# Weights of every other index of the seven-product stage arrive in four free slots instead of the weight ring

## The chip, the core and the metric

The kernel runs on one core of one Trainium2 chip. The metric is the device time of one launch in microseconds. The engines meant below are TensorE (PE, matrix products, with its weight loads shown as PEld), VectorE (DVE), ScalarE (ACT), GpSimd (POOL), and SyncE (SP), whose queue issues nearly all DMA transfers. Each engine takes its instructions strictly in the order in which they were built.

## The reference

One inference step of a two-layer decoder trunk over 1040 prompt rows (16 learned ones and 1024 of the prompt) and 8 sequences of 4 sample rows, with a model width of 1024. Layer 0 has an S5 scan beside a short gated convolution, layer 1 a Conformer convolution module, and both end in a gated feed-forward block of width 2816:

```
def conv_ffn(xn, fbuf, p, l):
    u = xn @ p['w_ffn_up'][l]
    a, g = jnp.split(u, [D_FF], axis=-1)
    a_c, nbuf = causal_dwconv(a, fbuf, p['w_ffn_conv'][l])
    return (jax.nn.silu(a_c) * g) @ p['w_ffn_down'][l], nbuf
```

All data is 32-bit. The kernel keeps that precision by cutting every matrix operand into a high and a low part (`h` is the operand rounded to the matmul type, `l` the rest) and computing three products: `xh*wh`, `xl*wh`, `xh*wl`.

## The kernel before

The rows are worked on in two halves: half 0 has 512 rows, half 1 has 560 (528 prompt rows and the 32 sample rows). The feed-forward width is cut into 22 indices `f` of 128 columns, in groups `GROUPS` of 2, 4, 4, 4, 4 and 4. For each index the kernel makes `a` and `g` (`up`), the three-tap convolution of `a`, `h = silu(conv) * g`, and splits `h`; when a group is complete, `down` adds its product with `w_down` to the residual `xr`, in eight output tiles `m`.

The change lies in the last stage, half 1 of layer 1. There `a` and `g` of an index come from one two-by-two block product with seven block products instead of eight (`up7`). The 1024 input rows are two blocks of 512, and the 560 rows of the half are two blocks of 280; `prepare` forms the combinations of the activations once (`oh`, `ol`). For each index the two raw weight tiles, value `w_up[2f]` and gate `w_up[2f+1]`, each 128x1024 (512 KB), are seen as four halves of 128x512: `a11`, `a12`, `a21`, `a22`. DVE forms from them `s1 = a21+a22`, `s2 = s1-a11`, `s4 = a12-s2`, `s3 = a11-a21`. Seven weights, `a11`, `a12`, `s1`, `s2`, `s3`, `s4`, `a22`, are each split: the high part by ACT (`wh`, or `a22h`), the low part by DVE (`wl`, `a22l`). That is `hl`, and every split is of 128x512.

The seven products of an index (`product`, twelve matmuls of 280 columns each) go into three PSUM banks: `bx` collects `a11*B11`, then `s2*T2`, then `s3*T3`, then `a22*N4`; `by` collects `s1*T1`, then `s4*B22`; `bz` holds `a12*B21`. A bank is read between two products, before the next one is added to it: after the first product ACT copies `bx` to the first half of `ap` (the evacuation of the first product, L908) and `by` to `g` (L910), after `s2` ACT copies `bx` to the second half of `ap` (L916, L917), after `s4` DVE adds `by` to it. Then ACT and DVE do the convolution (`c`, L499 on ACT and two L501 on DVE), ACT the silu (`s`, L926, L927). After `s3` DVE adds `bx` to `g`; only then may the `a22` product be added to that bank. After it DVE multiplies it into `s` and `split` makes `hh` and `hl`, the operands of `down`.

Raw weights come through a ring of two buffers, tag `raw`, 4 KB per partition each, which the tiles of `w_down` (also 512 KB) share in the order of the program. So an index takes both buffers, and its transfers can be issued only when the splits and sums of the previous user have read the buffers. Split weights live in rings `wh`, `wl` of three. `slot("v", ...)` gives one of eight slots of 584 numbers per partition; in this stage they hold `ap` and `c` of each index (and `h` of two indices of the last group); when the stage begins they still hold the operands of half 0's last `down`. Five banks, tag `mm`, serve `up7` (three per index) and `down` (two per `m`).

The order of instructions on each engine is set when the program is built: the framework's scheduler simulates the program with its own costs and due times, and whatever it finds ready first stands first in the queue. At run time nothing is reordered. The loop that calls `up7` is `run` with the hooks `out0` (final scaling and output of half 0, tile `xr`, L1167, L1168) and `finals` (the tail).

Of the kernel before, what the change touches and what calls it, by code (L numbers as in the profile page):

```python
# [12 lines left out]
F32 = mybir.dt.float32  # L13
# [8 lines left out]
P = 128  # L22
# [15 lines left out]
FT = FF // P  # L38
# [22 lines left out]
def grp(lo, hi, n):  # L61
    return [list(range(f, f + n)) for f in range(lo, hi, n)]


GROUPS = grp(0, 2, 2) + grp(2, FT, 4)


def build(nc, tc, ctx, a):
    sm = ctx.enter_context(tc.tile_pool(name="sm", bufs=1))
    sl = ctx.enter_context(tc.tile_pool(name="sl", bufs=1))  # L70
    wp = ctx.enter_context(tc.tile_pool(name="wp", bufs=3))
    ps = ctx.enter_context(tc.tile_pool(name="ps", bufs=1, space=PSUM))
    dr = ctx.enter_context(tc.tile_pool(name="dr", bufs=1, space=DRAM))
    V, A, PL, PE, SY = nc.vector, nc.scalar, nc.gpsimd, nc.tensor, nc.sync
    COUNT = {"x": NXT, "xh": NXH, "t": NTT, "v": NVT}

    def slot(tag, name, shape, dt=F32):
        if isinstance(shape, int):
            shape = [P, TN[shape]]
        n = math.prod(shape[1:])  # L80
        assert n <= SW
        t = sl.tile([P, SW], dt, tag=tag, name=name, bufs=COUNT[tag])
        v = t[:shape[0], :n]
        if len(shape) > 2:
            n = " ".join(f"d{i}" for i in range(len(shape) - 1))
            v = v.rearrange(f"p ({n}) -> p {n}", **{f"d{i}": shape[i + 1] for i in range(len(shape) - 2)})
        return v
# [4 lines left out]
    def bank(name, tag="aux"):  # L92
        return ps.tile([P, 512], F32, tag=tag, name=name, bufs=BANKS[tag])
# [6 lines left out]
    def tt(o, x, y, op, e=V):  # L100
        return e.tensor_tensor(o, x, y, op=op)  # L101
# [53 lines left out]
    def split(src, name, hf, scale=None, tag="xh", t0=0):  # L155
        hl = h, l = [slot(tag, name + c, hf, F32R) for c in "hl"]
        src, h, l = [t[:, t0:] for t in (src, h, l)]
        if scale is None:
            A.activation(h, src, AF.Copy)  # L159
            tt(l, src, h.bitcast(F32), SUB)  # L160
        else:
            A.activation(h, src, AF.Copy, scale=scale)  # L162
            V.scalar_tensor_tensor(l, src, scale, h.bitcast(F32), op0=MUL, op1=SUB)  # L163
        return hl
# [6 lines left out]
    def ntok(hf):  # L171
        return TN[0] if hf == 0 else HP1
# [3 lines left out]
    def tick(us, mark):  # L176
        state["f"] += us * RATE
        with tc.issue_after(mark.ins), tc.issue_after(state["pe"].ins):
            while fills and state["f"] >= 1:
                r = next(fills[0], "end")  # L180
                if r == "end":
                    fills.pop(0)
                elif r is False:
                    state["f"] = 1
                    return
                else:
                    state["f"] -= 1
# [215 lines left out]
    def sj(t, o=HP1):  # L403
        return t[:, o:o + NS * DS].rearrange("p (s j) -> p s j", j=DS)
# [93 lines left out]
    def conv3(dst, src, w, n):  # L498
        A.activation(dst[:, :n], src[:, 0:n], AF.Copy, scale=w[:, 0:1])  # L499
        for k in (1, 2):  # L500
            mk = V.scalar_tensor_tensor(dst[:, :n], src[:, k:k + n], w[:, k:k + 1], dst[:, :n], op0=MUL, op1=ADD)  # L501
        return mk

    def s6(t, n):
        return t[:, n:n + 6 * NS].rearrange("p (s j) -> p s j", j=6)

    def last2(t, n):
        return t[:, n - 6:n + 6 * NS].rearrange("p (s j) -> p s j", j=6)[:, :, 4:6]
# [268 lines left out]
    class FFN:  # L777
# [77 lines left out]
        def up7(self, f, tag, htag, stag, atag):  # L855


            fw, n, H = self.fw[:, f], ntok(1), self.H
            o, M = 2 + n, P * KT // 2
            raws = []  # L860
            for i in range(2):
                raw = wp.tile([P, 1024], F32, tag="raw", name="raw", bufs=2)
                SY.dma_start(raw, a["w_up"][(self.layer * FT + f) * 2 + i])
                raws.append(raw)

            def ring():
                return [wp.tile([P, 1024], F32R, tag=t, name=t, bufs=WB) for t in ("wh", "wl")]

            def hl(hl_, raw):
                A.activation(hl_[0], raw, AF.Copy)  # L870
                tt(hl_[1], raw, hl_[0].bitcast(F32), SUB)
                return hl_

            def halves(w):
                return [[t[:, i * M:(i + 1) * M] for t in w] for i in range(2)]

            (a11, a12), (a21, a22) = [(t[:, :M], t[:, M:]) for t in raws]
            w11, w12 = halves(ring())
            hl(w11, a11)
            s1, s2, s3, s4 = [slot(stag, "s%d" % i, [P, M]) for i in range(1, 5)]  # L880
            tt(s1, a21, a22, ADD)
            ws1, ws2 = halves(ring())
            hl(ws1, s1)
            hl(w12, a12)
            tt(s2, s1, a11, SUB)
            hl(ws2, s2)
            tt(s4, a12, s2, SUB)
            ws4, ws3 = halves(ring())
            hl(ws4, s4)
            tt(s3, a11, a21, SUB)  # L890
            hl(ws3, s3)
            w22 = hl([slot(atag, "a22" + c, [P, M], F32R) for c in "hl"], a22)

            def product(b, w, x, start):
                for k, xk in enumerate(self.ops[x]):
                    for i in range(3):
                        state["pe"] = PE.matmul(  # L897
                            b[:, :H], w[i == 2][:, k * P:(k + 1) * P], xk[i == 1],
                            start=(start and k == 0 and i == 0), stop=(k == KT // 2 - 1 and i == 2),
                            skip_group_check=True)  # L900

            bx, by, bz = [bank("mm", "mm") for _ in range(3)]
            ap = slot(tag, "ap", [P, o + 6 * NS])
            PL.tensor_copy(ap[:, 0:2], self.carry[:, f])
            PL.tensor_copy(s6(ap, o)[:, :, 0:2], self.fin[:, f])
            g = slot("t", "g", [P, H])
            product(bx, w11, "B11", True)
            A.activation(ap[:, 2:2 + H], bx[:, :H], AF.Copy)  # L908
            product(by, ws1, "T1", True)
            A.activation(g, by[:, :H], AF.Copy)  # L910
            product(bz, w12, "B21", True)
            tt(ap[:, 2:2 + H], ap[:, 2:2 + H], bz[:, :H], ADD)
            product(bx, ws2, "T2", False)
            m = n - H
            sa, sp = s6(ap, o)[:, :, 2:6], ap[:, 2 + H:o]
            A.activation(sp, bx[:, :m], AF.Copy)  # L916
            A.activation(sa, sj(bx, m), AF.Copy)  # L917
            product(by, ws4, "B22", False)
            tt(sp, sp, by[:, :m], ADD)
            tt(sa, sa, sj(by, m), ADD)  # L920
            PL.tensor_copy(self.fout[:, f], last2(ap, o))
            nc_ = n + 6 * NS
            c = slot(tag, "c", [P, nc_ + 2])
            conv3(c, ap, fw, nc_)
            s = slot("t", "s", 1)
            A.activation(s[:, :n], c[:, :n], AF.Silu)  # L926
            A.activation(sj(s), s6(c, o)[:, :, 0:4], AF.Silu)  # L927
            self.flush()
            product(bx, ws3, "T3", False)
            tt(g, g, bx[:, :H], ADD)  # L930
            tick(84 * H / 2400, tt(s[:, H:], s[:, H:], g, MUL))
            h = {}

            def rest():
                product(bx, w22, "N4", False)
                tt(s[:, :H], s[:, :H], bx[:, :H], MUL)
                h[1] = split(s, "h", 1, tag=htag)

            self.pend = rest
            return h  # L940
# [439 lines left out]
```

## Time and profile before

| | |
|---|---|
| runs | 2243.32 us median of 3 (2242.76 to 2243.97) |
| profiled execution, its own time | 2242.73 us |
| span of that execution | 2240.9 us |
| mean granted TensorE clock | 0.990 |
| PE busy / DVE busy / ACT busy / POOL busy | 98% / 76% / 37% / 33% |
| first and last matmul of `product` (L897) | 1821.3 to 2174 us |

The profile is of one execution. Its page gives busy shares by engine and by fortieth of the span; the trace behind it has every instruction with its start, its duration and, where its engine stood idle before it, how long and for which event. A bracket such as `[2.03 <-ACT wh L870]` behind a row means that the engine was idle 2.03 us before this instruction and that ACT's write of `wh` at line 870 ended the idle time. PE rows overlap: a 280-column matmul lasts 0.29 us but the next one starts about 0.13 us later.

### The profile page before, as it was taken

The numbers are of one execution on the slowest core, as the hardware profiler recorded it, in microseconds if no ns is written. First come the engines' busy times: TensorE is split into PE (matmuls) and PEld (weight loads), VectorE is DVE, ScalarE is ACT, GpSimd is POOL, SyncE is SP. The second block draws the span as 40 slices with busy tenths as digits, with TensorE's granted clock in tenths as the row PEclk, the third lists the DMA queues.
The fourth block names the chain that finished last, engine by engine and source line by source line (L and its number), as shares of the span: only waits on it lengthen the run. The fifth ranks groups of instructions, "written<-read, shape, count | busy, mean of one in ns | idle before, by whom it ended". The sixth has DMA issues, their size and how long they took to land.

```text
span 2240.9 us, 34315 instructions
## 1 busy us (share of the span) xinstructions
PE 2185.1 (98%) x13504; PEld 1982.3 (88%) x13504; DVE 1694.9 (76%) x2872; ACT 827.9 (37%) x1255; POOL 734.3 (33%) x632
## 2 busy tenths in 40 slices
PE   7999999999999999999999999999999997999997
PEld 6888898888888889999999998888887987999997
DVE  8979966545544678888896789899998387878784
ACT  5122354322332423232234523333335343455452
POOL 3212114323333434333443426455454401110011
PEclk8999999999999999999999999999999999999998
DMA  5234541223222332222222353232322222333231
GB/s 170 94 97 132 187 142 50 94 94 94 94 94 94 94 94 86 85 85 85 85 77 93 94 109 99 94 94 85 112 86 87 84 76 94 113 95 95 87 105 61
DMA packets 98338, 218.07 MB, mean 97 GB/s; under 512 B 28417, under 2 KB 45185, under 8 KB 98177
## 3 DMA queue, kind: packets, MB, share of 16 engines
q1 hardware_dynamic: 97632, 215.37, 31.1%
q8 instruction: 106, 1.74, 0.3%
q10 hardware_dynamic: 544, 0.52, 0.1%
q14 instruction: 56, 0.45, 0.1%
HBM read 202.49 MB, written 13.36 MB: 96 GB/s over the span
## 4 chain that ended last, share of the span: by engine, by line
PE 76%; DVE 13%; issue 3%; DMA 3%; ACT 2%; POOL 1%; SPq 1%; POOLq 0%; ACTq 0%; DVEq 0%
PE mm L145 66%; PE mm L897 8%; DVE c L501 2%; DVE wl L101 1%; DMA raw<-w_up 1%; DVE cvb L1052 1%; DVE cva L1052 1%; DVE xr L101 1%; DMA x<-x 1%; DVE xnl L163 1%; DMA raw<-w_down 1%; DVE hl L101 1%; ACT wh L113 1%; DVE s L101 1%; PE bcs L253 1%
## 5 line engine op out<-in xcount | busy, mean ns | idle before, releaser
L101 POOL TENSOR_TENSOR wl<-raw,wh 128x1024 fp32r<-128x1024 f32 x181 | 444.2, 2454 | 662.0 <-ACT wh L113 619.9
L145 PE MATMUL mm<-xnh,wh 128*128 128x280 f32 (+3 forms) x2176 | 637.7, 337 | 6.7 <-ACT xnh L162 6.7
L145 PE MATMUL mm<-xnl,wh 128*128 128x280 f32 (+3 forms) x2176 | 641.2, 338 | 2.5 <-DVE xnl L163 2.5
L145 PE MATMUL mm<-xnh,wl 128*128 128x280 f32 (+3 forms) x2176 | 639.3, 338 | 0.0
L113 ACT ACTIVATE wh<-raw 128x1024 fp32r<-128x1024 f32 x300 | 317.5, 1058 | 662.2 <-PE mm L145 580.6
L145 PEld LDWEIGHTS mm<-xnh,wh 128*128 128x128 f32 x2176 | 376.6, 189 | 47.5 <-ACT xnh L162 6.7
L145 PEld LDWEIGHTS mm<-xnl,wh 128*128 128x128 f32 x2176 | 375.6, 188 | 46.0 <-DVE xnl L163 4.2
L145 PEld LDWEIGHTS mm<-xnh,wl 128*128 128x128 f32 x2176 | 376.9, 189 | 40.3 <-issue 0.8
L145 PE MATMUL mm<-hh,wh 128*128 128x280 f32 (+2 forms) x992 | 288.6, 329 | 13.9 <-ACT hh L159 7.1
L145 PE MATMUL mm<-hl,wh 128*128 128x280 f32 (+2 forms) x992 | 288.7, 327 | 0.0
L145 PE MATMUL mm<-hh,wl 128*128 128x280 f32 (+2 forms) x992 | 287.2, 327 | 0.3 <-POOL wl L101 0.3
L101 DVE TENSOR_TENSOR xr<-mm,xr 128x280 f32<-128x280 f32 (+4 forms) x328 | 160.5, 515 | 118.9 <-PE mm L145 118.7
L101 DVE TENSOR_TENSOR wl<-raw,wh 128x1024 fp32r<-128x1024 f32 (+1 forms) x163 | 180.3, 1116 | 28.1 <-ACT wh L113 17.5
L145 PEld LDWEIGHTS mm<-hh,wh 128*128 128x128 f32 x992 | 174.3, 189 | 30.4 <-ACT hh L159 7.3
L501 DVE SCALAR_TENSOR_TENSOR c<-ap,fw,c 128x576 f32<-128x576 f32 (+2 forms) x176 | 170.0, 966 | 27.8 <-ACT c L499 25.4
L145 PEld LDWEIGHTS mm<-hl,wh 128*128 128x128 f32 x992 | 174.5, 189 | 14.3
L145 PEld LDWEIGHTS mm<-hh,wl 128*128 128x128 f32 x992 | 173.5, 189 | 14.9 <-POOL wl L101 0.7
L1052 DVE SCALAR_TENSOR_TENSOR cva<-vp,w_dw,cva 128x512 f32<-128x512 f32 x240 | 178.9, 746 | 0.0
L1052 DVE SCALAR_TENSOR_TENSOR cvb<-vp,w_dw,cvb 128x512 f32<-128x512 f32 x240 | 178.8, 746 | 0.0
L101 POOL TENSOR_TENSOR s<-s,g 128x512 f32<-128x512 f32 (+2 forms) x66 | 92.2, 1397 | 206.7 <-DVE g L101 176.8
L897 PE MATMUL mm<-oh,wh 128*128 128x280 f32 x528 | 154.4, 294 | 5.6 <-ACT wh L870 2.7
L897 PE MATMUL mm<-ol,wh 128*128 128x280 f32 x528 | 154.3, 294 | 0.0
(264 smaller groups left out, 3119.8 us busy)
## 6 DMA issues: line engine op xcount, KB each, us to landing
raw<-w_up SPq DMA_DIRECT2D x176, 512.0 KB
raw<-w_down SPq DMA_DIRECT2D x88, 512.0 KB
raw<-w_pw SPq DMA_DIRECT2D x48, 512.0 KB
raw<-w_in SPq DMA_DIRECT2D x22, 512.0 KB
raw<-w_out SPq DMA_DIRECT2D x12, 512.0 KB
du<-up SPq DMA_DIRECT2D x8, 292.0 KB
u<-du SPq DMA_DIRECT2D x32, 73.0 KB
x<-x SPq DMA_DIRECT2D x8, 280.0 KB
```

Source lines behind the costliest of these rows:

```text
L101: return e.tensor_tensor(o, x, y, op=op)
L113: A.activation(h, raw, AF.Copy)
L145: state["pe"] = PE.matmul(banks[b][:, :n_], wl if i == 2 else wh, xx[:, t0:t0 + n_], start=(k == 0 and i == 0), stop=(k == n - 1 and i == 2))
L163: V.scalar_tensor_tensor(l, src, scale, h.bitcast(F32), op0=MUL, op1=SUB)
L253: PE.matmul(b[:, c * w:(c + 1) * w], one1[:w], dg[:, c0 + c], start=True, stop=True)
L501: mk = V.scalar_tensor_tensor(dst[:, :n], src[:, k:k + n], w[:, k:k + 1], dst[:, :n], op0=MUL, op1=ADD)
L897: state["pe"] = PE.matmul(b[:, :H], w[i == 2][:, k * P:(k + 1) * P], xk[i == 1], start=(start and k == 0 and i == 0), stop=(k == KT // 2 - ...
L1052: V.scalar_tensor_tensor(b, v, w, b, op0=MUL, op1=ADD)
```

## The change

For odd `f` below 18 (nine of the 22 indices: 1, 3, ..., 17) the two raw tiles no longer take the ring. Each is loaded as two halves of 128x512 (256 KB) into slots of tag `v`: four slots and four transfers per index instead of two ring buffers and two transfers. Even indices, indices 18 to 21 and `w_down` use the ring as before. A pair of an even and an odd index then takes 2 + 6 = 8 `v` slots, so every role comes back to the slot it had in the pair before. The arithmetic is the same.

```
-                raw = wp.tile([P, 1024], F32, tag="raw", name="raw", bufs=2)
-                SY.dma_start(raw, a["w_up"][(self.layer * FT + f) * 2 + i])
+                src = a["w_up"][(self.layer * FT + f) * 2 + i]
+                if f % 2 and f < GROUPS[-1][0]:
+
+                    raw = [slot("v", "rw", [P, M]) for _ in range(2)]
+                    for j in range(2):
+                        SY.dma_start(raw[j], src[:, j * M:(j + 1) * M])
+                else:
+                    raw = wp.tile([P, 1024], F32, tag="raw", name="raw", bufs=2)
+                    SY.dma_start(raw, src)
+                    raw = [raw[:, :M], raw[:, M:]]
                 raws.append(raw)
...
-            (a11, a12), (a21, a22) = [(t[:, :M], t[:, M:]) for t in raws]
+            (a11, a12), (a21, a22) = raws
```

Lines below the change move by eight: L870, L897, L908, L916 of before are L878, L905, L916, L924 of the changed kernel. The scheduler, given other buffers, also writes another order for the stage. Numbers in the tile names below are the builder's counters.

First place, SP's queue at the start of the stage. Before, the transfers stand in the order of use: two `w_up` tiles each for index 0, 1 and 2, then `w_down` of the first group, then index 3.

```order
L863 DMA raw_17055<-w_up 128x1024
L863 DMA raw_17057<-w_up 128x1024
L863 DMA raw_17185<-w_up 128x1024
L863 DMA raw_17187<-w_up 128x1024
L863 DMA raw_17352<-w_up 128x1024
L863 DMA raw_17354<-w_up 128x1024
L110 DMA raw_17508<-w_down 128x1024
L110 DMA raw_17597<-w_down 128x1024
L863 DMA raw_17669<-w_up 128x1024
L863 DMA raw_17671<-w_up 128x1024
```

Now the tiles of index 2 (`raw_17356`, `raw_17358`) stand ahead of the four halves of index 1, and those of index 4 (`raw_17811`, `raw_17813`) ahead of the halves of index 3.

```order
L870 DMA raw_17055<-w_up 128x1024
L870 DMA raw_17057<-w_up 128x1024
L870 DMA raw_17356<-w_up 128x1024
L870 DMA raw_17358<-w_up 128x1024
L867 DMA rw_17185<-w_up 128x512
L867 DMA rw_17186<-w_up 128x512
L867 DMA rw_17189<-w_up 128x512
L867 DMA rw_17190<-w_up 128x512
L110 DMA raw_17512<-w_down 128x1024
L110 DMA raw_17601<-w_down 128x1024
L870 DMA raw_17811<-w_up 128x1024
L870 DMA raw_17813<-w_up 128x1024
```

What moved: the odd index's transfers now follow those of the next even index.

Second place, the seam from index 8 to index 9, on ACT. Before, `ap_18682` and `c_18754` are index 8's, `raw_18792` is index 9's raw tile, `wh_18796` its `a11`, `a12`, `wh_18805` its `s1`, `s2`, and `ap_18829` the evacuation of index 9's own first product.

```order
L870 ACTIVATE wh_18796<-raw_18792 128x512 x2
L870 ACTIVATE wh_18805<-s1_18800 128x512
L870 ACTIVATE wh_18805<-s2_18801 128x512
L916 ACTIVATE ap_18682<-mm_18679 128x248
L917 ACTIVATE ap_18682<-mm_18679 128x8x4
L870 ACTIVATE a22h_18822<-raw_18794 128x512
L499 ACTIVATE c_18754<-ap_18682,fw_13586 128x576
L870 ACTIVATE wh_18815<-s4_18803 128x512
L870 ACTIVATE wh_18815<-s3_18802 128x512
L908 ACTIVATE ap_18829<-mm_18826 128x280
```

Now, with `ap_18698`, `c_18770` of index 8, `rw_18808`, `rw_18809` (`a11`, `a12`), `wh_18825` (`s1`, `s2`) and `ap_18849` of index 9:

```order
L924 ACTIVATE ap_18698<-mm_18695 128x248
L925 ACTIVATE ap_18698<-mm_18695 128x8x4
L499 ACTIVATE c_18770<-ap_18698,fw_13586 128x576
L878 ACTIVATE wh_18816<-rw_18808 128x512
L878 ACTIVATE wh_18816<-rw_18809 128x512
L934 ACTIVATE s_18774<-c_18770 128x528
L935 ACTIVATE s_18774<-c_18770 128x32
L159 ACTIVATE hh_18790<-s_18644 128x560
L916 ACTIVATE ap_18849<-mm_18846 128x280
L878 ACTIVATE wh_18825<-s1_18820 128x512
```

What moved: all weight splits of index 9 went behind index 8's last evacuation and convolution step, and the split of `s1` behind the evacuation of index 9's own first product. The same two rows stand in this order at indices 1, 5, 9, 13 and 17, and at no other odd index.

On PE at the same seam, before, the last rows of index 8's `s3` product (`mm_18679`, weights `wh_18668`, `wl_18669`) are followed by index 9's `a11` product (`mm_18826`); index 8's `a22` product comes 31 matmuls later.

```order
L897 MATMUL mm_18679<-oh_16818,wh_18668 128x280
L897 MATMUL mm_18679<-ol_16819,wh_18668 128x280
L897 MATMUL mm_18679<-oh_16818,wl_18669 128x280
L897 MATMUL mm_18826<-oh_16763,wh_18796 128x280
L897 MATMUL mm_18826<-ol_16764,wh_18796 128x280
```

Now the `a22` product of index 8 follows its `s3` product in the same bank (`mm_18695`), and index 9's `a11` product (`mm_18846`) and `s1` product (`mm_18847`) come after that.

```order
L905 MATMUL mm_18695<-oh_16818,wh_18684 128x280
L905 MATMUL mm_18695<-ol_16819,wh_18684 128x280
L905 MATMUL mm_18695<-oh_16818,wl_18685 128x280
L905 MATMUL mm_18695<-oh_16775,a22h_18691 128x280
L905 MATMUL mm_18695<-ol_16776,a22h_18691 128x280
```

What moved: nothing stands any more between the two products of one bank. The same pair is adjacent at indices 0, 4, 8, 12 and 16.

Third place, PE from index 10 into `down` of its group. Before, eight matmuls of `down` (`mm_19092`, `mm_19093`) and the whole `s3` product follow the last row of index 10's `s4` product (`mm_18974`), then 24 more of `down`, and then its `a22` product.

```order
L897 MATMUL mm_18974<-oh_16814,wl_18963 128x280
L145 MATMUL mm_19092<-hh_18297,wl_19089 128x280
L145 MATMUL mm_19093<-hh_18297,wl_19089 128x280
L145 MATMUL mm_19092<-hh_18774,wh_19088 128x280
L145 MATMUL mm_19093<-hh_18774,wh_19088 128x280
```

Now `s3` stands ahead of `s4`, and four matmuls of `down` and the twelve of `a22` (`mm_18993`) follow; eleven more of `down` later comes `mm_19191`, the first in a bank that index 10 has to give up.

```order
L905 MATMUL mm_18994<-oh_16814,wl_18983 128x280
L145 MATMUL mm_19112<-hl_18942,wh_19108 128x280
L145 MATMUL mm_19113<-hl_18942,wh_19108 128x280
L145 MATMUL mm_19112<-hh_18941,wl_19109 128x280
L145 MATMUL mm_19113<-hh_18941,wl_19109 128x280
L905 MATMUL mm_18993<-oh_16775,a22h_18989 128x280
```

What moved: `s4`, on whose result the convolution waits, went behind `s3` and behind most of the `down` work that is ready early. Index 14 has the same order.

## The prediction

> **What bounds the kernel now.** I read the page first, then the busy time in stretches of the stage, then the rows in which PE stood idle there, and then what those waited for.
>
> ```profile
> span 2240.9 us, 34315 instructions
> PE 2185.1 (98%) x13504; PEld 1982.3 (88%) x13504; DVE 1694.9 (76%) x2872; ACT 827.9 (37%) x1255; POOL 734.3 (33%) x632
> ```
>
> PE is busy 98% of the span, so only the gaps of PE can be won, and any new gap is lost in full. By stretches of the stage (columns: us, then PE, PEld, DVE, ACT, POOL busy with counts, granted clock, DMA share, GB/s):
>
> ```profile
> 1820.00:1840.00 20.00, 17.97 (x122) 17.48 (x121) 17.33 (x32) 10.21 (x20) 2.19 (x4) 0.91 0.24 80
> 1840.00:1870.00 30.00, 23.91 (x168) 22.82 (x166) 20.23 (x44) 12.05 (x26) 4.63 (x7) 0.94 0.29 88
> 1870.00:1900.00 30.00, 23.65 (x167) 23.08 (x168) 25.13 (x47) 10.88 (x22) 3.88 (x5) 0.89 0.33 105
> 1900.00:1930.00 30.00, 29.89 (x230) 29.47 (x229) 28.69 (x53) 18.04 (x38) 3.10 (x7) 1.00 0.29 99
> 1930.00:1960.00 30.00, 28.42 (x220) 28.20 (x219) 18.99 (x37) 8.32 (x16) 5.58 (x5) 1.00 0.34 112
> 1960.00:1990.00 30.00, 30.00 (x235) 30.00 (x234) 26.03 (x49) 18.84 (x40) 1.41 (x6) 1.00 0.23 71
> 1990.00:2020.00 30.00, 30.00 (x236) 30.00 (x235) 20.51 (x40) 12.78 (x22) 6.16 (x8) 1.00 0.36 106
> ```
>
> PE's gaps lie at the start: 2.0 + 6.1 + 6.4 us up to 1900, at a clock of 0.89 to 0.94. From 1960 on PE is never idle, at 30.00/236 = 0.127 us per matmul. So from index 7 on the ring costs nothing now. The rows behind a gap:
>
> ```profile
> 1825.22 0.40 PE L897 MATMUL mm<-oh,wh 128*128 128x280 f32 x1 [2.03 <-ACT wh L870]
> 1856.36 0.40 PE L897 MATMUL mm<-oh,wh 128*128 128x280 f32 x1 [2.14 <-ACT ap L917]
> 1862.83 0.40 PE L897 MATMUL mm<-oh,wh 128*128 128x280 f32 x1 [0.39 <-ACT g L910]
> 1865.44 0.40 PE L897 MATMUL mm<-oh,a22h 128*128 128x280 f32 x1 [0.78 <-DVE g L101]
> 1874.70 1.53 PE L145 MATMUL mm<-hh,wh 128*128 128x280 f32 x5 [7.05 <-ACT hh L159]
> 1939.66 0.40 PE L145 MATMUL mm<-hh,wh 128*128 128x280 f32 x1 [1.58 <-DVE s L101]
> ```
>
> Two of them come from the ring: ACT, in order, stands before a transfer that got its buffer late.
>
> ```profile
> 1854.90 1.06 ACT L113 ACTIVATE wh<-raw 128x1024 fp32r<-128x1024 f32 x1 [2.98 <-DMA raw<-w_down]
> 1865.31 0.50 DVE L101 TENSOR_TENSOR ap<-ap,mm 128x248 f32<-128x248 f32 x2
> 1868.67 1.15 ACT L870 ACTIVATE wh<-raw 128x512 fp32r<-128x512 f32 x2 [5.89 <-DMA raw<-w_up]
> 1869.72 0.76 ACT L499 ACTIVATE c<-ap,fw 128x576 f32<-128x576 f32 x1
> ```
>
> Index 2's `ap` was complete at 1865.81, but its convolution step on ACT (`c`) had to wait until 1869.72 behind index 3's split, whose tile landed only then: 3.9 us of the 7.05. The 2.14 are the same with `w_down`.
>
> A gap can cost twice, since the clock halves after it:
>
> ```profile
> 1822.96:1826.37 3.41, 1.38 (x11) 1.15 (x11) 3.41 (x7) 2.22 (x5) 0.00 (x0) 1.00 0.00 0
> 1826.37:1829.79 3.42, 3.42 (x17) 3.42 (x16) 3.42 (x7) 1.59 (x3) 0.00 (x0) 0.50 0.23 42
> 1857.10:1860.51 3.41, 3.41 (x17) 3.41 (x16) 3.14 (x16) 0.42 (x1) 0.00 (x0) 0.50 0.51 154
> 1935.60:1939.02 3.42, 2.48 (x20) 2.26 (x18) 2.77 (x3) 1.22 (x3) 0.07 (x1) 1.00 0.31 71
> 1939.02:1942.43 3.41, 2.77 (x21) 2.77 (x22) 2.46 (x5) 1.46 (x4) 0.00 (x0) 1.00 0.22 90
> ```
>
> A stretch of 3.41 us with 2.03 us idle is followed by one at 0.50, in which PE did 17 matmuls where 26.9 fit: (26.9 - 17) x 0.127 = 1.3 us lost; the stretch after the 2.14 went the same way. The gap of 1.58 us fell across two stretches (0.94 and 0.64 idle) and halved nothing.
>
> A page's rule weighed against this: the Trainium skill, page "TensorE: Matmul & The Clock Gate", section "What's actually happening", has the clock go cold after an idle window of about 3.4 us. By that, gaps of 2 us would cost no clock, and the sum would be about 1.3 us smaller (C without its two stretches, D without the one that it saves). The trace disagrees (2.03 us were enough), and I go by the trace.
>
> **The change part by part.** Durations for the steps that follow:
>
> ```profile
> 1834.34 0.63 ACT L870 ACTIVATE wh<-s 128x512 fp32r<-128x512 f32 x1 [1.15 <-DVE s L101]
> 1835.55 0.38 ACT L908 ACTIVATE ap<-mm 128x280 f32<-128x280 f32 x1
> 1838.34 0.43 DVE L101 TENSOR_TENSOR g<-g,mm 128x280 f32<-128x280 f32 x1
> 1839.90 0.81 DVE L501 SCALAR_TENSOR_TENSOR c<-ap,fw,c 128x576 f32<-128x576 f32 x1
> 1841.85 0.64 ACT L926 ACTIVATE s<-c 128x528 f32<-128x528 f32 x1
> 1843.00 0.44 DVE L101 TENSOR_TENSOR s<-s,mm 128x280 f32<-128x280 f32 x1
> 1843.13 0.29 PE L897 MATMUL mm<-oh,wh 128*128 128x280 f32 x1
> ```
>
> *Transfers.* Bytes are the same; nine times two transfers become four, 18 more issues on SP, whose queue the next transfers pass anyway. SP is not what PE waits for, so zero, as long as halves land before their splits, which now stand late (second rival).
>
> *A, the seam of one bank.* At indices 0, 4, 8, 12 and 16 `a22` follows `s3` in the same bank, and DVE must add the bank to `g` between them. PE waits from the last matmul's issue slot to its result, 0.29 - 0.13, plus the 0.43 of `g` and two hand-overs of about 0.05: 0.7 us. The one such row of before is the 0.78. Where DVE has a `c` step (0.81) in hand, which I expect at 0 and 4, up to 1.3. Nothing covers it: the next index's products stand behind. Sum 3 x 0.78 + 2 x 1.3 = 4.9 us (ends 3.4 and 6.5).
>
> *B, the late splits.* At indices 1, 5, 9, 13 and 17 the split of `s1` stands on ACT behind the evacuation of the index's own first product, and PE's next product after that one is `s1`. So PE waits 0.29 - 0.13 + 0.38 + 0.63 = 1.17 us each time; that ACT rows overlap by 0.1 is made up by hand-overs. DVE's part (`c`, two `wl`, two `s`, then `s1`) ends at about the same time, so it cannot be less, and more where DVE has other work between: at index 5 the output scaling L1167 and splits of index 6 stand there, for which I add 1.0. Sum 5 x 1.17 + 1.0 = 6.9 us (5.0 to 8). Before, the splits were done an index earlier and nothing was waited for.
>
> *C, the way into `down`.* At index 10, after the last `s4` matmul, 4 + 12 + 11 = 27 matmuls (3.4 us) stand before the first that needs the bank of index 10. That bank is free when: result 0.29, `ap` 0.50, `c` 0.76 + 0.81 + 0.81, `s` 0.64, `s` times bank 0.44, six hand-overs of 0.05, and 0.4 more since a low split of `w_down` stands between: 4.95 us. A wait of 1.5, the same mechanism as the 1.58 of the row at 1939.66 (index 6); I take 1.58. Before, 8 + 12 + 24 + 12 = 56 matmuls (7.1 us) covered it at indices 10 and 14. At index 6 the new order has `s3` and 30 of `down` behind `s4`, so the old 1.58 goes. Each new gap is followed by a second one of the same kind or by a halved stretch, either about 1.3. Net 2 x (1.58 + 1.3) - 1.58 = 4.2 us (0 to 5.8).
>
> *D, the start.* Index 3 no longer uses the ring, so index 2's `c` starts when `ap` is there: -3.9, leaving about 3.2 of the 7.05. Index 2's tiles come earlier, so the 2.14 goes, and with it the halved stretch after it, -1.3. But `w_down` still shares the ring with index 2: its second tile waits for index 2's splits and ACT stands before it with index 2's `g` (L910) behind: the 0.39 there becomes about 1.8, +1.4. The 2.03 belongs to index 0, whose order is unchanged: 0. Sum -5.9 us; ends -9.5 (most of the 7.05 goes, and its clock) and -1.5 (other gaps follow).
>
> *Sum.* 4.9 + 6.9 + 4.2 - 5.9 = +10.1 us on a profiled execution of 2242.73 us (span 2240.9 and 1.8 around it), 0.6 below the median of 2243.32. Median: 2243.3 + 10.1, about 2253.5. Other stages keep their order.
>
> **Rivals.** *Faster: the ring is the only cost.* If seams A and B cost nothing because ACT and DVE run far enough ahead, only D is left, with all 9.5 us of it: 2234. It decides at a seam price of zero, that is when `s1` of indices 1, 5, 9, ... is split before PE ends the `a11` product. For it speak the 37% of ACT and that halves would land early; against it that both engines are in order and the row ahead is PE's own result. In its favour a page says that repeated gaps on the engine that should be saturated can mean too few buffers (the Trainium skill, "Perfetto Trace Analysis", "Optimization Strategy"); by that rule the result would be this rival's. The trace shows such gaps only up to 1940.
>
> *Much slower: the halves come late.* In SP's queue they stand behind two tiles of the next even index, which wait for buffers of the ring. If each of the nine waited for its data, with 2 MB in flight instead of 1:
>
> ```profile
> 1865.06 3.51 DMA raw<-w_up
> 1909.36 1.49 SPq L863 DMA_DIRECT2D raw<-w_up  x2
> 1910.52 4.30 DMA raw<-w_up
> ```
>
> Two tiles issued together took 4.30 where one took 3.5; four halves behind them add some 3 us, and where the splits need them at once each odd index loses about 1.5 more: 9 x 1.5 = 13, 2267. Against it: at index 9 the tiles of index 10 are released when index 8's sums are made, some 12 us before the splits of 9 stand.
>
> *No change.* A, B and C partly lie in each other's shadow (a gap lets DVE and ACT catch up, so that the next is shorter). If B falls to half and the second gaps of C don't come, 4.9 + 3.5 + 1.6 - 9.5 = 0.5: 2243.8.
>
> **How the numbers follow.** The forecast has 0.76, faster 0.07, no change 0.09, much slower 0.08. The range takes the ends that can meet: low 3.4 + 5 + 1.6 - 7 = +3.0, and high 6.5 + 8 + 5.8 - 3.5 = +16.8, so 2246.5 to 2260; it takes in part of the no-change case. Within 0.2% means within 4.5 us, about what a measurement of this kernel can tell from no change. Slower by more 0.83, within 0.10, faster 0.07.
>
> **What would show it.** A: five rows of PE `mm<-oh,a22h` with 0.7 to 1.3 <-DVE g. B: five of `mm<-oh,wh` with about 1.2 <-ACT wh (the split of `s1`). C: rows of L145 <-DVE s with about 1.6 in the third and fourth group, and none at index 6. D: the 7.05 <-ACT hh gone or below 4. In stretches after 1960 PE at 28 instead of 30.00 per 30 us in every group. I am wrong if those stretches stay full, or if the gaps end on a DMA.

## Result, and the profile after

The changed kernel takes 2258.06 us (median of 4 runs, 2255.88 to 2258.63) against 2243.23 us before: ratio 1.0064, 95% interval 1.0047 to 1.0081, so 14.8 us slower. The forecast was 2253.5 with a range of 2246.5 to 2260. Run again beside the last experiments the same kernel gave 1.0064 (1.0051 to 1.0077). The profiled execution took 2255.88 us, its span is 13.2 us longer than before's:

```profile
span 2254.1 us, 34335 instructions
PE 2186.9 (97%) x13504; PEld 1981.4 (88%) x13504; DVE 1700.9 (75%) x2872; ACT 828.4 (37%) x1255; POOL 739.7 (33%) x632
```

The work is the same, and PE's busy time grew by only 1.8 us. The stretches of the stage (same columns as ahead of the change):

```profile
1820.00:1840.00 20.00, 15.75 (x104) 14.98 (x103) 15.39 (x28) 9.63 (x20) 0.46 (x3) 0.91 0.31 106
1840.00:1870.00 30.00, 26.78 (x195) 26.15 (x195) 23.63 (x52) 15.86 (x32) 5.84 (x8) 0.94 0.34 105
1870.00:1900.00 30.00, 27.19 (x199) 26.96 (x199) 26.22 (x49) 10.38 (x23) 2.48 (x5) 0.94 0.28 90
1900.00:1930.00 30.00, 26.49 (x197) 25.37 (x196) 25.03 (x46) 15.82 (x32) 4.04 (x7) 1.00 0.31 98
...
1960.00:1990.00 30.00, 28.30 (x218) 27.84 (x217) 21.42 (x41) 16.26 (x36) 0.98 (x6) 1.00 0.22 71
1990.00:2020.00 30.00, 27.34 (x211) 26.88 (x210) 23.80 (x41) 13.39 (x24) 8.51 (x8) 1.00 0.46 141
2020.00:2050.00 30.00, 30.00 (x235) 30.00 (x234) 17.82 (x35) 10.75 (x23) 0.46 (x3) 1.00 0.22 71
2050.00:2080.00 30.00, 28.30 (x217) 27.84 (x216) 25.79 (x46) 17.51 (x34) 6.58 (x10) 1.00 0.26 86
```

Between 1840 and 1900 PE now does 394 matmuls where it did 335; from 1900 on it does 197 to 223 in all of these stretches but one, where it did 220 to 236. The gain at the start is there, and the later groups pay for it. What PE waited for in the stage (total us, times, longest):

```profile
PE mm L905 <- ACT wh L878: 8.0, 7, 2.0
PE mm L145 <- DVE s L101: 5.8, 4, 2.4
PE mm L145 <- DVE xr L101: 5.8, 4, 2.8
PE mm L905 <- DVE g L101: 4.5, 5, 1.2
PE mm L145 <- ACT wh L113: 1.4, 1, 1.4
```

None of these waits ends on a transfer. The rows behind them, among them one of ACT that belongs to the last:

```profile
1824.19 0.40 PE L905 MATMUL mm<-oh,wh 128*128 128x280 f32 x1 [2.03 <-ACT wh L878]
...
1834.95 0.40 PE L905 MATMUL mm<-oh,a22h 128*128 128x280 f32 x1 [1.21 <-DVE g L101]
1839.34 0.40 PE L905 MATMUL mm<-oh,wh 128*128 128x280 f32 x1 [1.01 <-ACT wh L878]
...
1866.73 0.60 PE L145 MATMUL mm<-hh,wh 128*128 128x280 f32 x1 [2.41 <-DVE s L101]
...
1873.61 0.60 PE L145 MATMUL mm<-hh,wh 128*128 128x280 f32 x1 [2.81 <-DVE xr L101]
...
1909.85 0.40 PE L905 MATMUL mm<-oh,wh 128*128 128x280 f32 x1 [1.32 <-ACT wh L878]
...
1938.37 0.40 PE L145 MATMUL mm<-hh,wh 128*128 128x280 f32 x1 [0.21 <-DVE s L101]
...
1944.12 0.40 PE L145 MATMUL mm<-hh,wh 128*128 128x280 f32 x1 [0.84 <-DVE xr L101]
...
1979.07 0.39 PE L905 MATMUL mm<-oh,a22h 128*128 128x280 f32 x1 [0.69 <-DVE g L101]
1979.30 0.29 PE L905 MATMUL mm<-ol,a22h 128*128 128x280 f32 x1
...
1983.45 0.40 PE L905 MATMUL mm<-oh,wh 128*128 128x280 f32 x1 [1.01 <-ACT wh L878]
...
2010.03 0.40 PE L145 MATMUL mm<-hh,wh 128*128 128x280 f32 x1 [1.60 <-DVE s L101]
2014.46 0.40 PE L145 MATMUL mm<-hh,wh 128*128 128x280 f32 x1 [1.06 <-DVE xr L101]
...
2177.57 1.06 ACT L113 ACTIVATE wh<-raw 128x1024 fp32r<-128x1024 f32 x1 [3.47 <-DMA raw<-w_down]
2178.68 0.40 PE L145 MATMUL mm<-hh,wh 128*128 128x280 f32 x1 [1.36 <-ACT wh L113]
```

The pair at 1979.07 and 1983.45 (a seam, A and B) comes again to the hundredth at 2052.58 and 2056.96 and at 2126.18 and 2130.55; the pair at 2010.03 and 2014.46 (the way into `down`, C) again at 2083.59 and 2088.02. The 2.03 is index 0's and unchanged. Behind the last row stands a transfer after all: ACT had waited 3.47 us for that tile of `w_down`, which comes through the ring. The seams have nothing of the kind.

One seam close up, in the rows of SP's queue, DVE and ACT (index 9, the halves `rw`; the row at 1981.71 is the sum `s1`):

```profile
1965.21 1.97 SPq L867 DMA_DIRECT2D rw<-w_up  x4
...
1976.42 0.51 DVE L101 TENSOR_TENSOR ap<-ap,mm 128x248 f32<-128x248 f32 x2 [3.70 <-PE mm L905]
...
1977.71 1.14 ACT L878 ACTIVATE wh<-rw 128x512 fp32r<-128x512 f32 x2
...
1981.71 0.68 DVE L101 TENSOR_TENSOR s<-rw 128x512 f32<-128x512 f32 x1
...
1982.47 0.41 ACT L916 ACTIVATE ap<-mm 128x280 f32<-128x280 f32 x1 [1.37 <-PE mm L905]
1982.77 0.62 ACT L878 ACTIVATE wh<-s 128x512 fp32r<-128x512 f32 x1
```

The four halves were issued by 1967.2, and the DMA engines, fully busy from 1968 to 1970, moved nothing from 1972 to 1978. The first split of them started at 1977.71 and did not wait for them. DVE even stood idle for 3.70 us before 1976.42, waiting for PE's `s4` product of index 8, with the sum `s1` of index 9 behind it in its queue. Then ACT evacuates index 9's first product (1982.47) and only after it splits `s1` (1982.77); PE starts on `s1` at 1983.45. That is late by order, not by data. The order on DVE counts as much as that on ACT: the sum `s1` itself was complete only at 1982.39, so with the split ahead of the evacuation PE would have started only about 0.3 us sooner (an estimate from these rows). In the kernel before, index 9's sum and split of `s1` started 11.6 and 6.5 us ahead of that evacuation:

```profile
1970.40 0.69 DVE L101 TENSOR_TENSOR s<-raw 128x512 f32<-128x512 f32 x1 [1.89 <-DMA raw<-w_up]
...
1975.49 1.16 ACT L870 ACTIVATE wh<-s 128x512 fp32r<-128x512 f32 x2 [0.21 <-PE mm L897]
...
1982.00 0.41 ACT L908 ACTIVATE ap<-mm 128x280 f32<-128x280 f32 x1
```

A table of the whole stage helps to place everything that follows: the start of the n-th matmul counted from the stage's first one, in each kernel's trace, less the same in before's trace. A column that stays level loses nothing there.

| n | place | change | e3 | e4 | e5 | e6 | e7 | e9 |
|---|---|---|---|---|---|---|---|---|
| 100 | seam 0 to 1 | +2.8 | 0.0 | 0.0 | 0.0 | +1.6 | 0.0 | -1.0 |
| 500 | group 1 in `down` | -4.9 | 0.0 | +0.1 | -4.9 | -5.3 | -4.6 | -5.7 |
| 600 | seam 4 to 5 | -0.4 | -0.3 | +0.2 | -4.2 | -5.2 | -4.5 | -6.1 |
| 800 | index 6, `down` | -0.7 | -0.3 | +2.1 | -3.6 | -5.3 | -4.6 | -7.6 |
| 1100 | seam 8 to 9 | +1.5 | +2.0 | +4.3 | -3.5 | -5.3 | -4.6 | -7.6 |
| 1300 | index 10, `down` | +4.7 | +3.9 | +7.6 | -0.7 | -5.3 | -4.6 | -7.6 |
| 1600 | seam 12 to 13 | +7.0 | +3.9 | +9.8 | -0.6 | -5.2 | -4.6 | -7.6 |
| 1900 | index 14, `down` | +10.3 | +3.9 | +13.0 | +2.1 | -5.2 | -4.6 | -7.6 |
| 2200 | seam 16 to 17 | +12.5 | +3.9 | +15.3 | +2.1 | -5.2 | -4.6 | -7.6 |
| 2581 | last product | +14.9 | +5.2 | +16.2 | +4.2 | -5.1 | -3.0 | -7.7 |

In the change's own profile the stage also began 1.0 us earlier than in before's, and the tail after it took 0.7 less: 14.9 - 1.0 - 0.7 = 13.2, the difference of the spans.

### The profile page after: what moved, and what is told of

It is laid out like the page before. It is cut to its first block, busy times and chain, and to the rows that moved or that the text cites. A ratio compares the mean times of both kernels' runs of the same rounds, so it can differ in the third digit from the quotient of the medians.

```text
span 2254.1 us, 34335 instructions
## 1 busy us (share of the span) xinstructions
PE 2186.9 (97%) x13504; PEld 1981.4 (88%) x13504; DVE 1700.9 (75%) x2872; ACT 828.4 (37%) x1255; POOL 739.7 (33%) x632
## 4 chain that ended last, share of the span: by engine, by line
PE 75%; DVE 14%; DMA 3%; issue 3%; ACT 2%; POOL 2%; SPq 0%; POOLq 0%; DVEq 0%; ACTq 0%
PE mm L145 66%; PE mm L905 7%; DVE c L501 2%; DVE wl L101 1%; DVE s L101 1%; DVE cvb L1060 1%; DVE cva L1060 1%; DVE xr L101 1%; DVE hl L101 1%; DVE xnl L163 1%; DMA raw<-w_down 1%; ACT wh L113 1%; DMA raw<-w_up 1%; DVE cv L101 1%; POOL wl L101 1%
## 5 line engine op out<-in xcount | busy, mean ns | idle before, releaser
L145 PEld LDWEIGHTS mm<-hh,wl 128*128 128x128 f32 x992 | 175.4, 190 | 14.9 <-POOL wl L101 0.7
L101 DVE TENSOR_TENSOR wl<-raw,wh 128x1024 fp32r<-128x1024 f32 (+1 forms) x145 | 169.0, 1172 | 22.6 <-ACT wh L113 17.9
L905 PE MATMUL mm<-oh,wh 128*128 128x280 f32 x528 | 154.6, 295 | 9.3 <-ACT wh L878 8.0
L905 PE MATMUL mm<-ol,wh 128*128 128x280 f32 x528 | 153.7, 293 | 0.0
```

What stands on the lines that cost most here:

```text
L145: state["pe"] = PE.matmul(banks[b][:, :n_], wl if i == 2 else wh, xx[:, t0:t0 + n_], start=(k == 0 and i == 0), stop=(k == n - 1 and i == 2))
L905: state["pe"] = PE.matmul(b[:, :H], w[i == 2][:, k * P:(k + 1) * P], xk[i == 1], start=(start and k == 0 and i == 0), stop=(k == KT // 2 - ...
```

## The experiments

Theory: the loss is the order of instructions that the builder wrote around the new buffers, at two kinds of place (the seam at the last index of a group, and the way into `down`). Rivals: the transfers themselves (smaller, more, later), the slots, or the start. All runs were timed beside the kernel before on the same chip (medians 2243.69, 2243.86 and 2244.01 us in the three sets).

**e1, the halves without the slots.**

```
                 if f % 2 and f < GROUPS[-1][0]:
-                    raw = [slot("v", "rw", [P, M]) for _ in range(2)]
+                    raw = wp.tile([P, 1024], F32, tag="raw", name="raw", bufs=2)
+                    raw = [raw[:, :M], raw[:, M:]]
```

> Odd indices below 18 load each raw tile as two transfers of 128x512, but into the ring as before; no slots. Theory (the loss is the built order: s1 of the last index of each group split behind that index's own first evacuation, and a22 put right behind s3 in the same bank): in the built order of this kernel neither occurs, so 2243.2 within 2 us, no A and no B gap. Rival 'eighteen more and smaller transfers cost' : most of the +14.8 us stays, 2250 or more. Rival 'the slots alone give the gain at the start': the 7.05 us wait ahead of the first down product stays in either case, since the ring is still shared.

Measured 2243.45 us, 0.9996 (0.9987 to 1.0005). Cutting a transfer in two costs nothing that can be measured here, and by itself it gains nothing. The wait ahead of the first `down` product stays too (7.65 us in its trace).

**e2, the slots at other indices**: 3, 7, 11, 15, none of them the last of its group.

```
-                if f % 2 and f < GROUPS[-1][0]:
+                if f % 4 == 3 and f < GROUPS[-1][0]:
```

> Slots and halves for indices 3, 7, 11, 15 only; 1, 5, 9, 13, 17 (each the last of its group) use the ring. Theory (built order): at no odd index is s1 split behind the own first evacuation and no a22 follows s3 in the same bank, so no A and no B; the start gets at most a little, 2239 to 2245. Rival 'halves in slots come late or cost something each': four of the nine indices are changed, so about 4/9 of +14.8, 2249 to 2250. Rival 'the start gains whenever index 3 leaves the ring': index 3 does leave it here, so 5 to 8 us faster, 2235 to 2238.

Measured 2247.07 us, 1.0015 (1.0006 to 1.0024): 3.4 us slower, above the range given, though the three seams after 1960 are whole: over those matmuls (n from 800 to 2200) its trace loses 1.0 us against before's, where the change loses 13.2. The one larger loss, 2.5 us, is a gap in `down` at index 6. The rival of the start fell too: index 3 is out of the ring and the wait is still there, since ACT, in order, has the silu of index 2 (L934) behind the splits of index 3, whose halves came late.

```profile
1871.20 0.63 ACT L878 ACTIVATE wh<-rw 128x512 fp32r<-128x512 f32 x1 [4.41 <-DMA rw<-w_up]
...
1872.64 0.63 ACT L934 ACTIVATE s<-c 128x528 f32<-128x528 f32 x1
...
1873.87 0.60 PE L145 MATMUL mm<-hh,wh 128*128 128x280 f32 x1 [6.10 <-DVE s L101]
```

In the change the silu stands ahead of those splits, and the wait for the first half is 0.43 us:

```profile
1865.55 0.64 ACT L934 ACTIVATE s<-c 128x528 f32<-128x528 f32 x1 [1.74 <-DVE c L501]
...
1867.30 1.22 ACT L878 ACTIVATE wh<-rw 128x512 fp32r<-128x512 f32 x2 [0.43 <-DMA rw<-w_up]
```

So taking index 3 out of the ring is not enough; in e6, where index 1 leaves it as well, the order is the change's and the wait is 2.40.

**e3, index 9 alone, and e4, indices 7 to 17.**

```
-                if f % 2 and f < GROUPS[-1][0]:
+                if f == 9:                                  # e3
+                if f % 2 and 6 < f < GROUPS[-1][0]:         # e4
```

> Slots and halves for index 9 alone. Theory: one A (0.69 and 0.16 of the result's pipeline), one B (1.01 and 0.16), and at index 10's way into down one C (1.60, and 1.06 if the second gap comes), each with 0.16: between +3.8 and +5.2, so 2247.0 to 2248.4. All other seams of the stage stay full and the start stays as before (7.05 us). Rival 'each changed index costs the same': +14.8 / 9 = 1.6, 2244.8. Rival 'the loss needs all slots in use': 2243.

> Slots and halves for odd indices 7 to 17; 1, 3 and 5 use the ring, so that the start is as before. Theory: three seams A and B (2.2 each with the pipeline's 0.16 twice) and two C (3.2 each, with second gaps) are 13.0, and up to 2.6 more at the end of the stage: 2256.2 to 2258.8, as slow as with all nine, because the gain at the start is missing. Rival 'each changed index costs the same': six of nine, +9.9, 2253. Rival 'the loss is at the start': 2243.

e3 measured 2246.80 us, 1.0014 (1.0005 to 1.0023), so +3.1; e4 2256.60 us, 1.0061 (1.0049 to 1.0074), so +12.9. One changed index brings the whole of a seam, and only there; the PE rows of e3 around it:

```profile
1938.12 0.40 PE L145 MATMUL mm<-hh,wh 128*128 128x280 f32 x1 [1.58 <-DVE s L101]
...
1979.32 0.39 PE L905 MATMUL mm<-oh,a22h 128*128 128x280 f32 x1 [0.69 <-DVE g L101]
1983.71 0.40 PE L905 MATMUL mm<-oh,wh 128*128 128x280 f32 x1 [1.01 <-ACT wh L878]
...
2010.31 0.40 PE L145 MATMUL mm<-hh,wh 128*128 128x280 f32 x1 [1.58 <-DVE s L101]
```

The 0.69 and 1.01 are those of the change to the hundredth; the first row is before's old gap at index 6. In the table e3 steps by 2.3 at that seam and by 1.9 at index 10, where the second gap of C did not come, and is level at the seams 12 to 13 and 16 to 17: 4.2, at the lower end of the 3.8 to 5.2 expected, where the timed difference is 3.1 (interval 1.1 to 5.2, so that the times alone would leave room for the 1.6 of the first rival; the place of the loss does not). At the last group e3's column rises by 1.3 more, with a gap of 1.06 us for a `wl`, which nobody expected. e4 has three such seams, two full C, 1.9 more at index 6 and no gain at the start: nearly as slow as the change with all nine.

**e5, the same nine indices, slots and halves, but the loads of an odd index stand one index earlier in the program** (in the call of the even index ahead of it).

```
+            if f % 2 and f < GROUPS[-1][0]:
+                raws = self.early
+            else:
+                raws = fetch(f)
+                if f + 1 < GROUPS[-1][0]:
+                    self.early = fetch(f + 1)
```

(`fetch` holds the loop over the two tiles as the change has it.)

> The same nine indices, the same halves and the same slots as the change, but the loads of an odd index stand in the program one index earlier (in the call of the even index ahead of it). In the order that is built from it, s1 of indices 1, 5, 9, 13, 17 is split ahead of the own first evacuation again and no a22 follows s3 in the same bank; the short way into down at indices 10 and 14 is still there. Theory (built order): A and B gone (-4.5 - 6.3 and 10 times 0.16 against the change), C stays (two times 1.60, with or without the second gap of 1.06), the start gains 5 to 8: 2239 to 2245. Rival 'the slots, the halves or their issues cost': nothing of that differs from the change, 2255 to 2259.

Measured 2247.35 us, 1.0015 (1.0006 to 1.0024): 10 us faster than the change with the same buffers and the same transfers. The seams at 9, 13 and 17 are gone (the column is level there). Index 10 still waits on its way into `down`, in two gaps:

```profile
2001.93 0.40 PE L913 MATMUL mm<-oh,a22h 128*128 128x280 f32 x1 [0.82 <-DVE g L101]
2006.22 0.40 PE L145 MATMUL mm<-hh,wh 128*128 128x280 f32 x1 [1.31 <-DVE s L101]
```

It missed the expected 2239 to 2245 because the start gained 4.9 and not up to 8, and because of losses that I had not counted: 0.7 at the seam 4 to 5 and 2.1 at the last group, both in gaps of 0.2 to 0.4 us, and 0.6 at index 6.

**e6, the start alone, and e7, the start with the loads written earlier.** e6 has `if f in (1, 3):`; e7 the same two indices with e5's edit.

> The change for indices 1 and 3 alone, order as built. Theory: the start as with the full change, A at index 0 and B at index 1 (+2.8 by the hundredth matmul of the stage), then -8.1 up to index 3, and before's stage from there: -4.9 against before, 2236 to 2241. Rival 'the gain at the start is given back at once, since the ring's next users wait instead' : 2243 to 2245.

> Slots and halves for indices 1 and 3 alone, and their loads stand one index earlier in the program. In the built order neither A at index 0 nor B at index 1 occurs. Theory: the gain of the start without the two gaps, -4.9 - 2.3 = -7.2, so 2234 to 2239, faster than before and than the start alone by 2 us. Rival 'the two gaps only make room, and the waits behind them grow by as much': the same time as the start alone, 2238 to 2240.

e6 measured 2239.30 us, 0.9979 (0.9971 to 0.9988); e7 2240.13 us, 0.9984 (0.9975 to 0.9992). e6 is what the theory said: with the seams of the later groups left out, the change is faster than before. e7 is not: A and B at indices 0 and 1 are gone (0.0 at n = 100), but nothing is left of it at n = 500, so the rival holds. PE comes to the next wait sooner, in e7 to the products of half 0's final norm (`bcs`):

```profile
1862.73 2.07 PE L253 MATMUL bcs<-dg,one 124*128 124x124 f32 x8 [4.41 <-DVE dg L101]
```

At the last group e7 loses another 1.5 us, with a gap of 1.27 for a `wl`, like the one of e3.

**e8 and e9, more of the start.** e8 is e7 with index 2 in slots too; e9 has indices 1 to 4 in slots and the loads of 1 to 6 written one index earlier.

```
+                    if f in (1, 2, 3, 4) and i in (0, 1):   # e9, in fetch
...
+            raws = self.early if f in (1, 2, 3, 4, 5, 6) else fetch(f)
+            if f + 1 in (1, 2, 3, 4, 5, 6):
+                self.early = fetch(f + 1)
```

> As the one before, and index 2 in slots as well, so that w_down of the first group has the ring for itself. Theory: the waits ahead of the first down products shrink further (2.41 and 2.81 in the changed kernel), by 1 to 2 us: 2233 to 2238. Rival 'the first down products wait for their operands, not for weights': same as the one before within 1 us.

> Indices 1, 2, 3 and 4 in slots, their loads and those of 5 and 6 written one index earlier. In the built order no late split of s1 at an odd index, no a22 right behind s3 in the same bank, and the first down product that needs index 6's bank stands later. Theory: the gap ahead of down at index 6 (1.58 and 0.16) goes too, which the kernel with three indices still had: 2234 to 2237. Rival 'it comes back elsewhere, as in the kernel with indices 1 and 3': 2237 to 2239.

e8 measured 2237.86 us, 0.9974 (0.9963 to 0.9984), e9 2234.64 us, 0.9959 (0.9946 to 0.9973): e9 is 9.4 us faster than before and the fastest kernel here. The gap at index 6 is gone, and its stretch is full:

```profile
1930.00:1960.00 30.00, 30.00 (x232) 29.79 (x232) 22.65 (x43) 10.82 (x20) 2.39 (x1) 1.00 0.27 89
```

e8 landed in its range, but not for the reason given: the waits ahead of the first `down` products did not shrink (2.47 and 2.11 against e7's 2.28 and 2.12), as its rival had it (whose time, within 1 us of e7's, was missed as well: e8's trace is ahead by 1.0 us at n = 100 and by 1.5 at the last group). Up to n = 2200 e9 is 3.1 us ahead of e7: 1.0 of it stands at n = 100, where its clock was not halved (last section), and 1.5 at index 6; the rest of the start is not told apart by order and clock.

**e10, the change once more.**

> The changed kernel once more, unchanged, for a tighter interval: 2255 to 2260. If its runs scatter by more than those of the kernel before, stretches at half clock that come or not (1.3 us each) are the nearest reason: the trace would show another number of them than four in the stage.

2257.58 us (2256.65 to 2260.58). Its runs scatter no more than those of the kernel before (3.9 against 4.4 us), and its trace has three halved stretches where the first has four. From 1900 on it has the same gaps within 0.04 us but for two. The one for `w_down` at the last group is 1.08, and no halved stretch follows. At index 6 it has 1.34 where the first profile has 0.21:

```profile
1941.53 0.40 PE L145 MATMUL mm<-hh,wh 128*128 128x280 f32 x1 [1.34 <-DVE s L101]
```

At the start a wait of 4.2 us for `xr` stands where the first profile has 2.81, and the gain there is 6.4 instead of 7.6 us.

## Why the prediction was right, step by step

The direction, the place and the three mechanisms were right; two sizes were low and one place was not named. That the time came within 4.6 us of the forecast is partly luck: the terms were off by +2.1, +2.0 and +1.7 one way and by -1.7 the other.

| step | forecast | in the change's trace (gaps, and by the table) |
|---|---|---|
| A and B, the seams | 4.9 + 6.9 = 11.8 | gaps 4.5 + 6.3 = 10.8; by the table 13.9 (2.77 + 4.46 + 2.19 + 2.25 + 2.26) |
| C, the way into `down` | +4.2 | 3.24 + 3.28 - 0.31 = +6.2 |
| D, the start | -5.9 | -7.6 (-6.4 in e10) |
| the last group | 0 | +2.4, then -0.7 in the tail |
| sum | +10.1 | +14.2 (the spans differ by 13.2, since the stage began 1.0 earlier) |

- **A** came at all five places, 1.21, 1.20 and three times 0.69 us idle, as reckoned (1.3 twice, 0.78 three times). The term was 0.9 low, since a gap costs more than its idle time. "Idle" in a row starts where the last matmul ends, 0.16 us after its issue slot is over (0.29 - 0.13); and the second matmul behind a gap starts 0.23 us after the first instead of 0.13, as the rows at 1979.07 and 1979.30 show. So each gap costs its idle time and 0.16 + 0.10, which makes A 4.5 + 5 x 0.26 = 5.8. The forecast's 1.17 for B had the 0.16 in it; A's 0.78, taken from a row, and C's 1.58 had not, and none had the 0.10.
- **B** came at all five places: 1.01 idle + 0.16 = 1.17 at four of them, the number forecast. That DVE's part ends at about the same time as ACT's was right too (1982.39 at index 9). At index 5 three gaps (1.32, 0.34, 0.64) came, 2.3 idle, where 1.17 + 1.0 was put. With 0.26 for each of the seven gaps B is 6.3 + 1.8 = 8.1 for 6.9. A and B together are then 13.9, what the table has.
- **C**: both new gaps are 1.60 (1.58 forecast) and the second ones 1.06 (1.3 forecast). The step that failed is "the old 1.58 goes": the gap at 1938.37 shrank to 0.21, but one of 0.84 for `xr` follows, and by the table only 0.3 was saved; in e10, with 1.34 and 0.84 there, nothing was saved and 0.8 was lost. The term ended above its end of 5.8. The halved stretch named as the other case did not come: 1.57 to 1.60 us idle in a stretch was too little.
- **D**: the 7.05 became 2.41, the 2.14 went, and index 2's `g` (L918), still behind a tile of `w_down`, costs PE 0.80 where 1.8 was put. A wait for `xr` that the prediction's rows leave out grew from 1.65 (the row of before below) to 2.81, and a stretch at half clock goes with the 2.41 and with the 2.81. The size is inside its ends. The reason given, that `c` of index 2 starts earlier once index 3 leaves the ring, was not enough: in e2 `c` did start as soon as `ap` was there, but the silu stood behind index 3's splits, and 6.10 us of wait remained.
- **The last group**, where no index is changed, was put at nothing ("Other stages keep their order" - but the order of these four indices changed too). A gap of 1.36 for a split of `w_down` and a halved stretch cost 2.4 in the first profile and 0.6 in e10, so this term is a matter of the run as well.

The row of before for `xr`:

```profile
1880.23 0.40 PE L145 MATMUL mm<-hh,wh 128*128 128x280 f32 x1 [1.65 <-DVE xr L101]
```

The faster rival (a seam price of zero) is excluded by e3, which bought one seam for 2.3 us. The much slower one (halves late) is excluded by the seam close up, and by e5: the same halves, without the loss. Slots at the start, where the gaps were, made e6 and e9 0.2% and 0.4% faster; from index 7 on, where PE had no gap before the last group, the same slots cost 12.9 us (e4). The faster rival leaned on the rule that repeated gaps on the engine that should be saturated can mean too few buffers (the Trainium skill, "Perfetto Trace Analysis", "Optimization Strategy"); it held where the gaps were.

What the runs don't settle is why the builder's order comes out so. e5 shows that the place of the loads in the program changes it; that the builder takes the halves to be late was not tried apart.

## What to carry to other kernels

Where a scheduler writes a static order, buffers are an input to that order: after adding some, compare the order of each engine's queue where PE was full before, above all for a product that lands right behind another in its own bank and for a split, or the sum it splits, that has slipped behind work of the unit before it. Add buffers first where the profile shows the gap; here indices 1 and 3 brought all of the gain, and 5, 9, 13 and 17 most of the loss. A load may move the queues of engines that never touch the transfer, and writing it a unit earlier in the program can put them back.

## What the runs showed of the hardware

The same gap costs more or less by where it falls against the grid of clock stretches. The 2.03 us ahead of index 0's `s1` product is in every kernel here. Where 1.92 us of it lie in one stretch of 3.41 us the next one runs at 0.50, in the change:

```profile
1822.27:1825.68 3.41, 1.49 (x11) 1.49 (x12) 3.41 (x7) 2.49 (x5) 0.00 (x0) 1.00 0.00 0
1825.68:1829.10 3.42, 3.42 (x17) 3.42 (x16) 3.32 (x6) 1.34 (x4) 0.00 (x0) 0.50 0.32 85
```

and where a border leaves 1.75 of it in the stretch, in e6, it does not:

```profile
1825.62:1829.03 3.41, 1.66 (x13) 1.66 (x14) 3.41 (x7) 2.33 (x5) 0.00 (x0) 1.00 0.00 0
1829.03:1832.45 3.42, 3.42 (x29) 3.42 (x28) 3.14 (x6) 1.79 (x4) 0.00 (x0) 1.00 0.36 101
```

About 1.2 us of time lie between the two (+2.8 against +1.6 at n = 100 in the table, with the same two gaps A and B behind). In the stage's profiles a full-clock stretch with 1.90 us idle or more was always followed by half clock. Below that most were not (1.75 in e6, 1.81 in e9, 1.84 in e7), but one of 1.79 in the change and one of 1.03 in e1 were, so idle time in the stretch alone does not decide it. Which side a gap falls on changes from run to run (the change's stretch of 1.79 has 1.27 in e10, and full clock behind it), and is a likely part of the 2 to 8 us by which runs of one kernel differ; that was not measured by itself. The Trainium skill ("TensorE: Matmul & The Clock Gate", "What's actually happening") asks for an idle window of about 3.4 us before the clock drops; here 1.9 us in a stretch of that length was enough.
